# A hybrid encoder block on one core: cumulated decays loaded from DRAM to all partitions, in place of one-hot products

## The chip, the cores and the metric

The kernel runs on one core of one Trainium2 chip. The metric is the device time of one execution in microseconds (us). TensorE multiplies, VectorE and ScalarE work on SBUF and PSUM, GpSimd on SBUF alone, and SyncE (SP) issues nearly all DMAs, in order.

## The reference, cut to what matters

One layer over x of 512 positions by 1024 channels, float32. Beside a pooling branch, eight heads of a gated delta rule run forward and backward, each with its own decay; a convolutional feed-forward part follows.

```python
h = rmsnorm(x, norm1_w[l])
proj = h @ w_in[l]
p, q, k, v, z, bf, bb, af, ab, g_pool, g_dn = jnp.split(proj, SPLIT_POINTS, axis=-1)
...
g_f = -jnp.exp(a_l[0]) * jax.nn.softplus(af.astype(f32) + dtb[0])
g_b = -jnp.exp(a_l[1]) * jax.nn.softplus(ab.astype(f32) + dtb[1])
o_f = gated_delta_rule(qc, kc, vc, g_f, beta_f)
o_b = flip(gated_delta_rule(flip(qc), flip(kc), flip(vc), flip(g_b), flip(beta_b)))
...
# inside gated_delta_rule, by chunks
G = jnp.cumsum(g, axis=-1)
diff = G[..., :, None] - G[..., None, :]
decay = jnp.where(incl, jnp.exp(jnp.minimum(diff, 0.0)), 0.0)
attn = jnp.einsum('bhnid,bhnjd->bhnij', q, k) * decay
qg = q * jnp.exp(G)[..., None]
```

The kernel works with chunks of 128 positions, four to a direction. For each head and direction it needs G (the cumulated decay) of the column position in every row: a row of 512 numbers spread over 128 partitions.

## The kernel before, in words

**How the work is laid out.** Every step is declared as a task with an engine, an estimated cost, the names it reads and writes and a key (`A`, `V`, `G`, `M`, `L` for ScalarE, VectorE, GpSimd, TensorE and SP's loads). A planner (`Planner.run`) simulates the engines with these costs: at each moment an engine takes the ready task with the smallest key whose buffers are free, and a ScalarE task that would change the activation table stands back for 2.0 us. The order it finds is emitted as it stands, so a changed cost, buffer count or dependence re-orders the whole program. `RINGS` says how many buffers each ring has (`ds`: three PSUM banks for short products; `r4`: four SBUF tiles of 4 KB per partition; `q`, `v`, `f`, `ext` and more); rings in the second argument are handed out in the order of declaration. Weight work has the smallest keys (`FEED`), then evictions (`EVICT`), then the delta chain (`CHAIN`); projections with plain keys fill TensorE in between.

**Projections.** Each unit of 128 output columns loads 512 KB of weights, ScalarE rounds them to a high part (L393), GpSimd makes the low part (L397), and TensorE adds 8 x 3 products of 128 x 512 (`mm3`, L372 to L374): the split format, fp32r. Products of the delta chain are plain fp32, 128 columns each.

**The decays.** `gate_unit` cumulates the log decays with triangular matrices and keeps G by token (`g_all`), split into a high and a low part (`g_hl`, L670 and L671). Four transposes (`row_turn`, L677) and a copy to `g_rows` (L680) give 32 rows of 512 positions: 16 high, 16 low, one for each head and direction. `decay_unit` then spreads one row at a time to all partitions: a one-hot matrix `pick`, whose column r has ones at rows r and r + 16, is the weight (L711):

```python
pe.matmul(gb[d], pick[:, r : r + 1].to_broadcast([32, P]), g_rows, start=True, stop=True)
```

From this PSUM bank VectorE makes the argument of the decay for each chunk (L718: plus neg_g, at most the mask) into an `r4` tile, ScalarE makes the exponentials of G for the queries (`qexp`, L726) from the same bank, and the decays themselves in place (`dexp`, L729).

**What follows.** `mats_unit` multiplies k by k and by the decays (L836, L844) and stores 32 x 32 blocks to DRAM (L855); `inv_unit` inverts these blocks on VectorE, `spread_unit` loads them back, `merge_unit` joins them. `delta_unit` runs two heads and both directions in four steps (L1109 to L1170). `fin_unit` norms and gates a head's output and splits it into high and low parts (L1262, L1265). Heads 0 to 3 (group 0) go first, then heads 4 to 7, whose decays reuse the `r4` tiles of the first group. In between TensorE works on the z, q, v, k and gate projections. `p_unit` makes the pooled maps `pm` (in `r4` tiles, L1355), `po_unit` and `do_unit` the two output projections; then come `w_o`, the up projection and the down projection.

Of the kernel before, what the change touches and what calls it, by code (L numbers as in the profile page):

```python
# [14 lines left out]
P = 128  # L15
S = 512
# [21 lines left out]
class Planner:  # L38
# [48 lines left out]
    def run(self):  # L87
# [33 lines left out]
        while todo:  # L121
# [6 lines left out]
            while again:  # L128
                again = False
                for e, q in queue.items():  # L130
# [3 lines left out]
                    for t in q:  # L134
# [3 lines left out]
                        rank = (turn and now - t.ready < 2.0, t.key, t.i)  # L138
# [35 lines left out]
                    for s in t.succs:  # L174
# [4 lines left out]
                        if not n.left:  # L179
                            queue.setdefault(n.eng, []).append(n)  # L180
                            heapq.heappush(events, max(now, n.ready))
                            if n.tab:
                                heapq.heappush(events, n.ready + 2.0)
# [25 lines left out]
def hybrid_block(  # L209
# [33 lines left out]
        "pp": 3, "ds": 3, "oo": 1, "raw": 3, "whi": 2, "wlo": 2, "y": 5, "f": 5, "z": 1, "q": 4, "v": 3,  # L243
# [38 lines left out]
    def f32(ap):  # L282
        return ap.bitcast(F32)
# [24 lines left out]
    pick = const.tile([32, 16], F32R, name="pick")  # L308
    pool.tensor_tensor(out=pick, in0=ident[0:32, 0:16], in1=ident[0:32, 16:32], op=ALU.add)
# [163 lines left out]
    g_hl = tok.tile([P, 4, 2, 16], F32R, name="g_hl")  # L473
    g_rows = tok.tile([32, S], F32R, name="g_rows")
# [124 lines left out]
    def gate_unit(box, pp):  # L599
# [72 lines left out]
        V(0.85, keep, r=["ds:gsum"], w=["g_all", "g_hl"], key=c)  # L672
# [6 lines left out]
        M(0.5, row_turn, r=["g_hl"], w=["ds:grow"], key=c)  # L679
        A(ca(512), lambda: act.copy(g_rows, gt["pr"][0:32, :]), r=["ds:grow"], w=["g_rows"], key=c)  # L680
# [24 lines left out]
    def decay_unit(h, c):  # L705
        gb = [None, None]

        def spread(d):
            gb[d] = bank("ds", f"gb_{h}{d}")
            r = 2 * h + d  # L710
            pe.matmul(gb[d], pick[:, r : r + 1].to_broadcast([32, P]), g_rows, start=True, stop=True)  # L711

        def arg(d):
            if dts[h] is None:
                dts[h] = r4(f"dt_{h}")
            for t in range(NT):
# [13 lines left out]

# [1213 lines left out]
```

## Time and profile before

| what | us |
|---|---|
| median of 3 runs (902.24 to 907.81) | 902.29 |
| profiled execution | 903.34 |
| its span, from first to last instruction | 901.5 |
| TensorE busy in the span | 887.5 |
| VectorE / ScalarE / GpSimd busy | 539.4 / 458.9 / 503.2 |

Busy time counts a moment once however many matmuls are under way; a matmul's own duration is longer than the distance to the next one, since they are pipelined. Where the price of a matmul is wanted, the distance between starts is to be read.

### The profile page before, as it was taken

Reading aid. Unit: us, or ns where it says so; the run is one execution under the profiler, and the core shown is the slowest. Engines: PE = TensorE matmul, PEld = TensorE weight load, DVE = VectorE, ACT = ScalarE, POOL = GpSimd, SP = SyncE. Lnnn points to the kernel's source line nnn. Section 1 sums busy time; section 2 is a strip of 40 time slices with the busy share of each in tenths; the row PEclk is TensorE's granted clock in tenths of the full one; section 3 lists DMA queues with packets and bytes.
Section 4 is the critical chain, followed back from the end, with each engine's and each line's share of the span. In section 5 each row is a group of like instructions: output and inputs, shape, how many; then the busy total and the mean of one; then the engine's idle time right before and its main releaser. Section 6 shows DMA issues by size and latency. Waiting matters only on the chain.

```text
span 901.5 us, 14144 instructions
## 1 busy us (share of the span) xinstructions
PE 887.5 (98%) x5194; PEld 739.0 (82%) x5194; DVE 539.4 (60%) x985; ACT 458.9 (51%) x791; POOL 503.2 (56%) x452
## 2 busy tenths in 40 slices
PE   8999999999999999999999999999999999999997
PEld 7878888788888877988888888878888888888876
DVE  4766684338877845564234244665655554579996
ACT  6688534428777343355544333534443333455654
POOL 3434555124375451366567905787778774566663
PEclk9999999999999999999999999999999999999999
DMA  6333548122245381131898606566665563265554
GB/s 204 97 110 106 135 113 200 52 71 71 54 130 133 115 204 35 47 87 60 250 325 264 191 21 213 172 212 221 219 212 198 201 209 103 95 210 176 184 175 152
DMA packets 175033, 135.97 MB, mean 151 GB/s; under 512 B 31942, under 2 KB 143347, under 8 KB 174964
## 3 DMA queue, kind: packets, MB, share of 16 engines
q1 hardware_dynamic: 174388, 134.02, 48.6%
q8 instruction: 41, 0.67, 0.3%
q10 hardware_dynamic: 576, 1.05, 0.3%
q14 instruction: 28, 0.23, 0.1%
HBM read 109.88 MB, written 25.17 MB: 150 GB/s over the span
## 4 chain that ended last, share of the span: by engine, by line
PE 86%; DVE 4%; DMA 3%; POOL 2%; SPq 2%; issue 1%; ACT 1%; POOLq 0%; DVEq 0%; ACTq 0%
PE ps_up L373 8%; PE ps_up L374 8%; PE ps_up L372 8%; PE dn L373 3%; PE dn L374 3%; PE dn L372 3%; PE ps_gd L372 2%; PE ps_z L372 2%; PE ps_k L372 2%; PE ps_q L372 2%; PE ps_k L374 2%; PE ps_k L373 2%; PE ps_do L374 2%; PE ps_wo L374 2%; PE ps_wo L372 2%; PE ps_wo L373 2%
## 5 line engine op out<-in xcount | busy, mean ns | idle before, releaser
L397 POOL TENSOR_TENSOR wl_up<-wr_up,wh_up 128x512 fp32r<-128x512 f32 x88 | 114.8, 1326 | 51.0 <-ACT wh_up L393 48.6
L374 PE MATMUL ps_up<-h_hi,wl_up 128*128 128x512 f32 (+1 forms) x368 | 139.9, 380 | 1.0 <-POOL wl_up L397 1.0
L373 PE MATMUL ps_up<-h_lo,wh_up 128*128 128x512 f32 (+1 forms) x368 | 139.9, 380 | 0.3 <-DVE h_lo L543 0.3
L372 PE MATMUL ps_up<-h_hi,wh_up 128*128 128x512 f32 (+1 forms) x368 | 140.0, 380 | 0.0
L1665 DVE SCALAR_TENSOR_TENSOR c<-ps_up,fw,c 128x511 f32<-128x511 f32 x88 | 66.0, 750 | 98.7 <-ACT c L1659 92.6
L1846 POOL TENSOR_TENSOR w_dn<-wr_dn,w_dn 128x512 fp32r<-128x512 f32 x44 | 65.2, 1493 | 35.9 <-ACT w_dn L1843 33.5
L1650 POOL TENSOR_TENSOR tp<-tp 128x512 f32<-128x512 f32 x44 | 61.4, 1395 | 41.4 <-DMA tp<-in_ffn_down_dram 38.5
L374 PEld LDWEIGHTS ps_up<-h_hi,wl_up 128*128 128x128 f32 x368 | 69.2, 188 | 14.5 <-POOL wl_up L397 1.4
L373 PEld LDWEIGHTS ps_up<-h_lo,wh_up 128*128 128x128 f32 x368 | 69.2, 188 | 13.5 <-DVE h_lo L543 0.5
L372 PEld LDWEIGHTS ps_up<-h_hi,wh_up 128*128 128x128 f32 x368 | 69.2, 188 | 13.3
L393 ACT CAST wh_up<-wr_up 128x1024 fp32r<-128x1024 f32 x44 | 46.3, 1052 | 62.7 <-issue 21.8
L1843 ACT CAST w_dn<-wr_dn 128x512 fp32r<-128x512 f32 x69 | 40.4, 618 | 41.1 <-DMA wr_dn<-in_ffn_down_dram 16.9
L373 PE MATMUL dn<-w_dn,as 128*128 128x512 f32 x141 | 54.6, 387 | 2.0 <-DVE w_dn L1846 1.9
L374 PE MATMUL dn<-w_dn,as 128*128 128x512 f32 x141 | 54.2, 385 | 0.0
L372 PE MATMUL dn<-w_dn,as 128*128 128x512 f32 x141 | 54.2, 385 | 0.0
L1619 DVE TENSOR_TENSOR as<-a,as 128x512 fp32r<-128x512 f32 (+1 forms) x41 | 38.9, 983 | 1.4 <-ACT as L1615 1.4
L397 POOL TENSOR_TENSOR wl_gp<-wr_gp,wh_gp 128x512 fp32r<-128x512 f32 x16 | 21.2, 1346 | 33.2 <-ACT wh_gp L393 33.2
L1615 ACT CAST as<-a 128x512 fp32r<-128x512 f32 (+1 forms) x41 | 21.5, 534 | 29.1 <-DVE a L1686 28.3
L397 POOL TENSOR_TENSOR wl_k<-wr_k,wh_k 128x512 fp32r<-128x512 f32 x16 | 20.2, 1285 | 26.4 <-ACT wh_k L393 22.0
L397 POOL TENSOR_TENSOR wl_v<-wr_v,wh_v 128x512 fp32r<-128x512 f32 x16 | 20.3, 1293 | 24.4 <-ACT wh_v L393 24.4
L1659 ACT ACTIVATE c<-ps_up,fw 128x512 f32<-128x512 f32 x44 | 33.9, 771 | 0.0
L397 POOL TENSOR_TENSOR wl_do<-wr_do,wh_do 128x512 fp32r<-128x512 f32 x16 | 25.0, 1586 | 15.1 <-ACT wh_do L393 15.1
(357 smaller groups left out, 2443.9 us busy)
## 6 DMA issues: line engine op xcount, KB each, us to landing
wr_up<-in_ffn_up_dram SPq DMA_DIRECT2D x44, 512.0 KB, 3.8
tp<-in_ffn_down_dram SPq DMA_DIRECT2D x22, 512.0 KB, 5.3
t_scr<-tp SPq DMA_DIRECT2D x44, 256.0 KB, 3.0
wr_dn<-t_scr SPq DMA_DIRECT2D x20, 512.0 KB, 4.0
wr_dn<-in_ffn_down_dram SPq DMA_DIRECT2D x15, 512.0 KB, 3.7
x<-in_x_dram SPq DMA_DIRECT2D x8, 512.0 KB, 5.3
wr_k<-in_w_in_dram SPq DMA_DIRECT2D x8, 512.0 KB, 5.5
wr_z<-in_w_in_dram SPq DMA_DIRECT2D x8, 512.0 KB, 4.1
```

Source lines behind the costliest of these rows:

```text
L372: pe.matmul(ps, ahi, bhi, start=first, stop=False)
L373: pe.matmul(ps, ahi, blo, start=False, stop=False)
L374: pe.matmul(ps, alo, bhi, start=False, stop=last)
L393: act.copy(b["hi"], b["raw"])
L397: pool.tensor_tensor(out=b["lo"][:, sl], in0=b["raw"][:, sl], in1=f32(b["hi"][:, sl]), op=ALU.subtract)
L1615: act.copy(sets[p][:, i : i + n, 0, :], src())
L1619: dve.tensor_tensor(out=w[:, :, 1, :], in0=src(), in1=f32(w[:, :, 0, :]), op=ALU.subtract)
L1650: G(cp(512), lambda o=o, x=x, y=y: pool.tensor_tensor(out=w(*o), in0=w(*x), in1=w(*y), op=ALU.subtract), r=[n(*x), n(*y)], w=[n(*o)], key=u)
L1659: act.activation(b[j], box["ps"], AF.Identity, scale=fw[:, 1, ci : ci + 1], bias=fw[:, 3, ci : ci + 1])
L1665: dve.scalar_tensor_tensor(out=y[:, lo:hi], in0=box["ps"][:, lo + sh : hi + sh], scalar=fw[:, k, ci : ci + 1], in1=y[:, lo:hi], op0=ALU.mu ...
L1843: act.copy(b["w"][:, 0, :], raw["t"][:, j, :])
L1846: eng.tensor_tensor(out=b["w"][:, 1, :], in0=raw["t"][:, j, :], in1=f32(b["w"][:, 0, :]), op=ALU.subtract)
```

## The change: what it does

`g_hl`, `pick` and the one-hot products go. The four transposes turn `g_all` itself (16 rows); the copy goes to a tile of the `f` ring, from which SP stores the rows to DRAM (`g_scr2`, one store for the forward direction, four for the backward one, whose chunks are turned round). Each `decay_unit` then loads its head's two rows to all 128 partitions straight into the `r4` tile (512 KB); `qexp` reads that tile, and the argument overwrites it. Besides: `pm` 2 and 3 share a tile of the `ext` ring instead of `r4` tiles; heads 6 and 7 take their sums in `fin_unit` on VectorE instead of GpSimd; rings `f` 5 to 6, `q` 4 to 3, `v` 3 to 4; and the planner's delay of table changes is 3.0 instead of 2.0 us.

```diff
-                        rank = (turn and now - t.ready < 2.0, t.key, t.i)
+                        rank = (turn and now - t.ready < 3.0, t.key, t.i)
...
-        "pp": 3, "ds": 3, "oo": 1, "raw": 3, "whi": 2, "wlo": 2, "y": 5, "f": 5, "z": 1, "q": 4, "v": 3,
+        "pp": 3, "ds": 3, "oo": 1, "raw": 3, "whi": 2, "wlo": 2, "y": 5, "f": 6, "z": 1, "q": 3, "v": 4,
...
-    pick = const.tile([32, 16], F32R, name="pick")
-    pool.tensor_tensor(out=pick, in0=ident[0:32, 0:16], in1=ident[0:32, 16:32], op=ALU.add)
...
-    g_hl = tok.tile([P, 4, 2, 16], F32R, name="g_hl")
-    g_rows = tok.tile([32, S], F32R, name="g_rows")
+    g_scr2 = dram.tile([H, 2, NT, P], F32, name="g_scr2")
...
-            dve.tensor_copy(hl[:, :, 0, :, :], g_all)
-            dve.tensor_tensor(out=hl[:, :, 1, :, :], in0=g_all, in1=f32(hl[:, :, 0, :, :]), op=ALU.subtract)
...
-                pe.transpose(pt[0:32, s * P : (s + 1) * P], f32(g_hl[:, s]).rearrange("p x r -> p (x r)"), ident)
+                pe.transpose(pt[0:16, s * P : (s + 1) * P], g_all[:, s].rearrange("p h d -> p (h d)"), ident)
+
+        def store_rows():
+            g_rows = gt["g"]
+            for d in range(2):
+                for s in range(NT) if d else (None,):
+                    if d:
+                        sp.dma_start(g_scr2[:, d, NT - 1 - s, :], g_rows[d::2, s * P : (s + 1) * P])
+                    else:
+                        sp.dma_start(g_scr2[:, d].rearrange("h t c -> h (t c)"), g_rows[d::2, :])
...
+        A(ca(512), keep_rows, r=["ds:grow", "pool:dp"], w=["f:grows"], key=c)
+        add("sp", 2.2, store_rows, ["f:grows"], ["g_scr2"], c, None, 32.0)
...
-        def spread(d):
-            gb[d] = bank("ds", f"gb_{h}{d}")
-            r = 2 * h + d
-            pe.matmul(gb[d], pick[:, r : r + 1].to_broadcast([32, P]), g_rows, start=True, stop=True)
+        def spread():
+            dts[h] = r4(f"dt_{h}")
+            sp.dma_start(dts[h], g_scr2[h].partition_broadcast(P))
...
-                    out=dts[h][:, d, t, :], in0=gb[d][:, s * P : (s + 1) * P], scalar=neg_g[:, s, h, d : d + 1],
+                    out=dts[h][:, d, t, :], in0=dts[h][:, d, t, :], scalar=neg_g[:, s_of(d, t), h, d : d + 1],
...
-            act.activation(qes[h][:, d].rearrange("p s c -> p (s c)"), gb[d][:, P:], AF.Exp)
+            src = dts[h][:, 0, 1:4] if d == 0 else dts[h][:, 1, 2::-1]
+            act.activation(qes[h][:, d], src, AF.Exp)
...
+        L(512, spread, r=["g_scr2"], w=[f"r4:dt{h}"], key=c)
         for d in range(2):
-            M(0.35, lambda d=d: spread(d), r=["g_rows", "pool:dp"],
-              w=[f"ds:gb{h}{d}", f"r4:dt{h}#{d}", f"qe:{h}#{d}"], key=c)
-            V(4 * cd(128), lambda d=d: arg(d), r=[f"ds:gb{h}{d}", "neg_g"], w=[f"r4:dt{h}#{d}"], key=c)
-            A(ca(384), lambda d=d: qexp(d), r=[f"ds:gb{h}{d}", "pool:dp"], w=[f"qe:{h}#{d}"], key=c, tab="exp")
+            A(ca(384), lambda d=d: qexp(d), r=[f"r4:dt{h}#{d}", "pool:dp"], w=[f"qe:{h}#{d}"], key=c, tab="exp")
+            V(4 * (cd(128) + 0.12), lambda d=d: arg(d), r=["neg_g"], w=[f"r4:dt{h}#{d}"], key=c)
...
+        E, cost, eng = (G, cp(512), pool) if h < H - 2 else (V, cd(512), dve)
...
+    pmn = [f"ext:pm#{g}" if g > 1 else f"r4:pm{g}" for g in range(4)]
...
+            if g > 1:
+                if not pmx:
+                    pmx["t"] = ring("dp", "ext", (P, 2, 2, S), F32R, "pm_x")
+                pm[g] = pmx["t"][:, 3 - g]
+            else:
+                pm[g] = r4(f"pm_{g}", (P, 2, S), F32R)
```

## Rows read from the trace of the kernel before

**Rows 1.** Page, parts 1 and 2: busy us, share and count; granted clock.
```profile
PE 887.5 (98%) x5194; PEld 739.0 (82%) x5194; DVE 539.4 (60%) x985; ACT 458.9 (51%) x791; POOL 503.2 (56%) x452
...
PEclk9999999999999999999999999999999999999999
```

**Rows 2.** Three stretches: length, busy us and count by engine, clock, DMA share, GB/s.
```profile
0.00:25.00 25.00, 22.33 (x141) 19.20 (x141) 11.08 (x20) 15.24 (x30) 10.21 (x57) 0.93 0.61 186
25.00:875.00 850.00, 845.89 (x4944) 704.06 (x4944) 508.66 (x929) 432.35 (x740) 482.20 (x389) 1.00 0.49 149
875.00:901.50 26.50, 19.23 (x111) 15.78 (x109) 19.64 (x37) 11.29 (x22) 10.83 (x7) 0.98 0.49 166
```

**Rows 3.** TensorE's timeline, 49.4 to 52.3 us: start, duration, line, tiles, shape, count.
```profile
49.48 0.39 PE L374 MATMUL ps_z<-h_hi,wl_z 128*128 128x512 f32 x1
49.80 0.73 PE L711 MATMUL gb<-g_rows,pick 32*128 32x512 f32 x2
50.46 0.50 PE L372 MATMUL ps_z<-h_hi,wh_z 128*128 128x512 f32 x1
50.80 0.39 PE L373 MATMUL ps_z<-h_lo,wh_z 128*128 128x512 f32 x1
51.03 0.40 PE L374 MATMUL ps_z<-h_hi,wl_z 128*128 128x512 f32 x1
51.35 0.49 PE L711 MATMUL gb<-g_rows,pick 32*128 32x512 f32 x1
51.77 0.50 PE L372 MATMUL ps_z<-h_hi,wh_z 128*128 128x512 f32 x1
52.11 0.40 PE L373 MATMUL ps_z<-h_lo,wh_z 128*128 128x512 f32 x1
```

**Rows 4.** Tile gb: count, ns min/median/max, first and last start in us, shape.
```profile
L718 DVE SCALAR_TENSOR_TENSOR dt<-gb,neg_g,mask x64: 319/343/351, 51.0 to 253.4; 128x128 f32<-128x128 f32 x64
...
L711 PE MATMUL gb<-g_rows,pick x16: 392/490/497, 49.8 to 250.1; 32*128 32x512 f32 x16
```

**Rows 5.** TensorE's timeline behind plain fp32 products, near 63 and 67 us.
```profile
62.80 0.48 PE L372 MATMUL ps_q<-h_hi,wh_q 128*128 128x512 f32 x1
63.12 0.40 PE L373 MATMUL ps_q<-h_lo,wh_q 128*128 128x512 f32 x1
...
67.29 0.49 PE L711 MATMUL gb<-g_rows,pick 32*128 32x512 f32 x1
67.70 0.50 PE L372 MATMUL ps_z<-h_hi,wh_z 128*128 128x512 f32 x1
68.04 0.40 PE L373 MATMUL ps_z<-h_lo,wh_z 128*128 128x512 f32 x1
```

**Rows 6.** DMA issues: tiles, queue, count, size, median us to landing.
```profile
z_scr<-zo SPq DMA_DIRECT2D x8, 256.0 KB, 2.0
...
n2b<-in_norm_w_dram SPq DMA_DIRECT2D x1, 512.0 KB, 6.6
nfb<-in_final_norm_w_dram SPq DMA_DIRECT2D x1, 512.0 KB, 4.3
```

**Rows 7.** Tile dt: the users of the finished decays, and their exponentials.
```profile
L844 DVE SCALAR_TENSOR_TENSOR nm<-pk,nbp,dt x64: 333/342/353, 63.2 to 270.9; 128x128 f32<-128x128 f32 x64
L729 ACT ACTIVATE dt<-dt x16: 614/630/650, 56.3 to 259.5; 128x512 f32<-128x512 f32 x16
```

**Rows 8.** Tiles wr_v and ps_v: issue of v's weights, and their first products.
```profile
L388 SPq DMA_DIRECT2D wr_v<-in_w_in_dram x8: 368/378/390, 49.2 to 306.0; - x8
...
L372 PE MATMUL ps_v<-h_hi,wh_v x64: 388/389/486, 73.2 to 331.1; 128*128 128x512 f32 x64
```

**Rows 9.** TensorE's timeline: last products of the second delta pair.
```profile
241.04 1.06 PE L1170 MATMUL o<-dt,w 128*128 128x128 f32 x8
```

**Rows 10.** Tile ob: a VectorE instruction with two operands in SBUF.
```profile
L1252 DVE SCALAR_TENSOR_TENSOR ob<-ob,small,zs x8: 744/1043/1798, 202.9 to 424.4; 128x512 f32<-128x512 f32 x8
```

**Rows 11.** Tile o_lo: a head's low part, and the output projection that reads it.
```profile
L373 PE MATMUL ps_do<-o_lo,wh_do x64: 389/389/398, 452.8 to 496.0; 128*128 128x512 f32 x64
L1265 POOL TENSOR_TENSOR o_lo<-ob,o_hi x8: 1272/1289/1760, 222.5 to 436.3; 128x512 fp32r<-128x512 f32 x8
```

More of the change, by code (lines that the diff above doesn't have):

```diff
@@ L182, in run @@
                             if n.tab:
-                                heapq.heappush(events, n.ready + 2.0)
+                                heapq.heappush(events, n.ready + 3.0)
         return sorted(ts, key=lambda t: (t.start, t.i))
@@ L676, in row_turn, with keep_rows @@
             for s in range(4):
-                pe.transpose(pt[0:32, s * P : (s + 1) * P], f32(g_hl[:, s]).rearrange("p x r -> p (x r)"), ident)
-        M(0.5, row_turn, r=["g_hl"], w=["ds:grow"], key=c)
-        A(ca(512), lambda: act.copy(g_rows, gt["pr"][0:32, :]), r=["ds:grow"], w=["g_rows"], key=c)
+                pe.transpose(pt[0:16, s * P : (s + 1) * P], g_all[:, s].rearrange("p h d -> p (h d)"), ident)
[7 more added lines that the diff above has]
+                        sp.dma_start(g_scr2[:, d].rearrange("h t c -> h (t c)"), g_rows[d::2, :])
+        M(0.5, row_turn, r=["g_all"], w=["ds:grow"], key=c)
+        def keep_rows():
+            gt["g"] = ring("dp", "f", (16, S), F32, "g_rows")
+            act.copy(gt["g"], gt["pr"][0:16, :])
+        A(ca(512), keep_rows, r=["ds:grow", "pool:dp"], w=["f:grows"], key=c)
+        add("sp", 2.2, store_rows, ["f:grows"], ["g_scr2"], c, None, 32.0)
         def rest():
@@ L1230, in fin_unit @@
         A(ca(512), square, r=[n("o")], w=[n("sq")], key=c)
-        G(cp(512), lambda: pool.tensor_tensor(out=b["sq"], in0=b["sq"], in1=b["a"], op=ALU.add),
-          r=[n("a")], w=[n("sq")], key=c)
+        E, cost, eng = (G, cp(512), pool) if h < H - 2 else (V, cd(512), dve)
+        E(cost, lambda: eng.tensor_tensor(out=b["sq"], in0=b["sq"], in1=b["a"], op=ALU.add), r=[n("a")], w=[n("sq")], key=c)
         def part():
@@ L1239, in rest @@
             b["lo"] = f_tile("osl", F32R)
-            pool.tensor_tensor(out=b["lo"], in0=b["sq"], in1=f32(b["hi"]), op=ALU.subtract)
+            eng.tensor_tensor(out=b["lo"], in0=b["sq"], in1=f32(b["hi"]), op=ALU.subtract)
         def total():
@@ L1247, in fin_unit @@
         A(ca(512), part, r=[n("sq")], w=[n("hi")], key=c)
-        G(cp(512), rest, r=[n("sq"), n("hi")], w=[n("lo")], key=c)
+        E(cost, rest, r=[n("hi"), n("sq")], w=[n("lo")], key=c)
         M(0.55, total, r=[n("hi"), n("lo")], w=[f"ds:pm{h}"], key=c)
@@ L1269, in hybrid_block @@
     pm = [None] * 4
+    pmx = {}
+    pmn = [f"ext:pm#{g}" if g > 1 else f"r4:pm{g}" for g in range(4)]
     def p_unit(g):
@@ L1350, in pmap @@
             mm3(b["p2"], b["w"][:, 0], b["w"][:, 1], b["yhi"], b["ylo"], True, True)
-        M(MM3, pmap, r=[f"pwr:{g}", f"y:yh{g}", f"y:yl{g}"], w=[f"ds:pw{g}", f"r4:pm{g}"], key=u)
+        M(MM3, pmap, r=[f"pwr:{g}", f"y:yh{g}", f"y:yl{g}"], w=[f"ds:pw{g}", pmn[g]], key=u)
         def sc_hi():
-            pm[g] = r4(f"pm_{g}", (P, 2, S), F32R)
+            if g > 1:
[4 more added lines that the diff above has]
+                pm[g] = r4(f"pm_{g}", (P, 2, S), F32R)
             act.activation(pm[g][:, 0, :], b["p2"], AF.Copy, scale=small[:, g : g + 1])
@@ L1362, in sc_lo @@
             )
-        A(ca(512), sc_hi, r=[f"ds:pw{g}", "small"], w=[f"r4:pm{g}"], key=u)
-        V(cd(512), sc_lo, r=[f"ds:pw{g}"], w=[f"r4:pm{g}"], key=u)
+        A(ca(512), sc_hi, r=[f"ds:pw{g}", "small"], w=[pmn[g]], key=u)
+        V(cd(512), sc_lo, r=[f"ds:pw{g}"], w=[pmn[g]], key=u)
     def po_unit(c):
@@ L1369, in po_unit @@
             pool_out[0][:, c * P : (c + 1) * P], 4, lambda k: (pm[k][:, 0, :], pm[k][:, 1, :]),
-            lambda k, a, b_: [f"r4:pm{k}"], f"po{c}",
+            lambda k, a, b_: [pmn[k]], f"po{c}",
         )
@@ L1597, in hybrid_block @@
     tail = [b for b in plan.owner if b.split(":")[0] == "y" or b[:3] in ("mhi", "mlo", "woh", "wol") or b[:2] in ("kT", "kk")]
-    tail += [n for n in ("beta", "xg", "neg_g", "neg_eg", "kdec", "gl", "g_rows", "g_hl")]
+    tail += [n for n in ("beta", "xg", "neg_g", "neg_eg", "kdec", "gl")]
     Z(ffn_open, w=["pool:fp"], after=tail)
```

7 lines of the change are left out of this document (1 added, 6 removed).

## The prediction

> **What bounds the kernel.** I read the page's busy shares first, then the stretches, then single matmuls. TensorE is busy 887.5 of 901.5 us, VectorE 60%, ScalarE 51%, GpSimd 56% [rows 1], and its granted clock stands at the higher of its levels (2.4 GHz) in nearly every slice. A busy share alone proves little, since busy time of pipelined matmuls overlaps; so the reader should see where the 14.0 us of idle time lie. By the three stretches [rows 2] 2.7 us lie in the first 25 us (the start: loads, first norm), 7.3 us after 875 (last matrix weights and the tail), and only 850.0 - 845.9 = 4.1 us in the 850 us between. In that long middle TensorE's queue is full. A second check is the distance between starts: matmuls of 512 columns follow each other every 0.23 us (50.80 to 51.03 [rows 3]). So a microsecond of matmul work taken from the middle is a microsecond of time, as long as the remaining work is there when its turn comes, and an engine beside it matters only if it makes TensorE wait.
>
> **What the change removes from TensorE.** The one-hot products: sixteen matmuls (8 heads, 2 directions) of 32 rows by 512 columns, between 49.8 and 250.1 us [rows 4]. Their own duration (0.49) is not their price; the distances are. One alone [rows 3]: its predecessor starts at 51.03, it at 51.35, the next product at 51.77, the one after at 52.11. From 51.03 to 52.11 are 1.08 us where two ordinary steps take 0.46: price 0.62. The queue loses 0.09 before it, 0.19 in it and 0.11 in the product behind it. A pair [rows 3]: 49.48 to 50.80 is 1.32, less 0.46, so 0.86 for two. One that follows another plain fp32 product [rows 5]: from its start at 67.29 to the second start after it, 68.04, are 0.75; less one step of 0.23, and less the 0.09 that a change from fp32 to the split format costs even without it (62.80 to 63.12 is 0.32, not 0.23), leaves 0.43. The timeline has eleven alone, one behind fp32 work, and two pairs, the second of them behind fp32 work (0.65 by the same reduction): 11 x 0.62 + 0.43 + 0.86 + 0.65 = 8.8 us. The four transposes that turn the cumulated decays into rows stay (16 columns each where 32 were), and nothing is added to TensorE. Sum on TensorE: -8.8 us.
>
> A page of the notes says otherwise. The Trainium skill, TensorE: Matmul & The Clock Gate, Why this matters for your kernels, holds that a single matmul over 32 rows takes as long as one over 128; by that each product costs one step of 0.23, the sixteen 3.7 us, and the time would be 898.6. The same skill's TensorEngine Tiling (Array Packing), Key Properties, says that a change of tiling mode drains the engine, which agrees with the 0.09 and 0.11 lost on either side. Measured distances decide for 0.62.
>
> **What it adds, and what covers it.** Five small stores on SP (one of 16 KB, four of 4 KB), then eight loads that copy a head's two 2 KB rows to 128 partitions, 512 KB each. No such load is in the trace before. The nearest rows are the two norm weights spread by the same kind of load: 4.3 and 6.6 us to landing; a store takes 2.0 [rows 6]; an issue on SP some 0.3 to 0.6. Group 0 (heads 0 to 3): rows ready at 49.5 by the first product's start; five issues 2.5, landing 2.0, issue 0.4, load 4.3 to 6.6 put the first decays at 58.7 to 61.0, where before they stood in PSUM at 50.3: 8.4 to 10.7 us later. Heads follow at the rate of the queue. The first use of a finished decay is at 63.2 [rows 7], so the first mats may slip a few us; but the fourth head's mats wait for its own k product late in the stage, so the inversion starts when it did. I take 0 for group 0; the bound is the full 10.7. While SP stands at the wait for the five stores, weight loads queue behind it. Their cover: the weights of the first v product are issued at 49.2 and first multiplied at 73.2 [rows 8], so a hold of 5 us costs 0. Without that cover a late weight load would stop TensorE for as long as it is late.
>
> Group 1 (heads 4 to 7): the buffer of the third pair comes free when the second delta pair ends, near 242.1 (241.04 + 1.06 [rows 9]). With issue and load, heads 6 and 7 have theirs at 246.8 to 249.1 instead of the first product at 243.4. ScalarE's query exponentials now stand before VectorE's decay arguments, because those overwrite the loaded tile: some 0.5 us more per direction. The last decay exponential starts at 259.5 and the last mats at 270.9 [rows 7], which leaves some 10 us of cover. I take 0, with 12 us as the bound of the delay.
>
> VectorE's 64 arguments (0.343 each [rows 4]) now read two operands in SBUF rather than one in PSUM. The nearest row with two SBUF operands, of 512 columns, runs from 0.744 to 1.798 [rows 10], a factor of 2.4. Bounds: 0, or 64 x 0.343 x 1.4 = 31 us of VectorE time over both groups; VectorE is 60% busy, and I take a third of it, hidden. The Trainium skill, SBUF — State Buffer, Who interferes with whom, gives the reason to expect the upper part: a Vector instruction with two SBUF inputs contends with a GpSimd instruction that reads SBUF. The spread of that row agrees.
>
> The eight loads move 4.2 MB; the queues are half used in the middle (DMA share 0.49 [rows 2]): 0.
>
> **What it moves.** Last two heads' squares and splits go from GpSimd to VectorE, the first two mapped pool groups into the freed `ext` buffer, a fourth v slot for a q slot, a sixth f slot, and the planner waits 3 rather than 2 us before it changes the activation table. None changes TensorE's work. They matter through the slack at the end of the delta stage: the last head's low part is done at 436.3 + 1.3 = 437.6, its consumer's stage begins at 452.8 [rows 11], and it is needed some 21 products (4.8 us) later. With TensorE 8.8 us earlier that slack is still 452.8 + 4.8 - 8.8 - 437.6 = 11 us. I take 0 for all; they re-lay the whole order, so the 4.1 us of idle in the middle may double or vanish, which is the main uncertainty: +-4.1.
>
> **Sum.** Profiled execution 903.34 (span 901.5): -8.8 gives 894.5. It lies 1.05 above the median 902.29, so against the median 893.5. From the idle in the middle I take 0.3 off (pool maps no longer wait for decay buffers): 893.2.
>
> **Rivals.**
> 1. The re-laid order gives back what was won: new waits of about 4 to 5 us, that is, the idle of the middle doubled. For: the planner re-times every engine with estimated costs, and loads that it cannot time exactly enter the chain. Against: TensorE has work queued throughout. Time 893.2 + 4.5 = 897.7.
> 2. A product is worth only its step and the drains turn up elsewhere: 16 x 0.23 = 3.7 us, so 902.29 - 3.7 = 898.6. For: the new order may put other changes of format where the products stood. Against: the distances of [rows 3] hold the drains beside the products. The page on the clock gate cited above stands for this case.
> 3. Slower: the delay of the decay chain reaches the end of the delta stage. Mechanism: loads on SP and slower arguments start the inversions late, o's last head arrives late, TensorE stands in front of the output projection. Price: delay D less the 11 us of slack; it decides from D = 20, where 893.2 + 9 is the time before. Only both groups at their upper bounds, adding up (10.7 + 12 = 23 us), give 893.2 + 12 = 905. Against: group 0's delay should end at the k products.
> 4. The order gets better: the 4.1 us of idle in the middle go: 889.4.
>
> **How the numbers follow.** Forecast 0.68 (its own range 890 to 896.5, with idle and drains a few us either way), rival 1 0.15, rival 2 0.05, rival 3 0.07, rival 4 0.05. A measurement of this kernel tells about 1% from no change, that is 893.3 or less is faster: half of the forecast's weight and rival 4 lie below, so faster 0.50; same takes the other half, rivals 1 and 2: 0.43; slower, rival 3: 0.07. Range 888.8 to 899.5: both bounds of the idle time, and rivals 1, 2 and 4, without 3.
>
> **What would show it.** Right: no products with 32 rows; the starts of the neighbouring products 0.23 apart there; TensorE's busy time near 878.5; idle in the middle near 4; eight loads of 512 KB landing in 4 to 7 us; the first output-projection product near 444. Wrong: TensorE idle before the merges or the output projection with a load, a decay or a late head as its releaser; weight loads that land after their turn; or the same busy time with more changes of format.

## The result, and the profile after

The changed kernel takes 897.89 us (median of 7 runs, 896.0 to 899.66) against 902.29 us: a ratio of 0.9936, interval 0.9915 to 0.9957. That is 4.4 us less, where the forecast said 9.1. The profiled execution took 899.28 us, 1.4 above its median. By the page (busy us, share, count) and the three stretches of [rows 2]:

```profile
PE 877.8 (98%) x5178; PEld 737.0 (82%) x5178; DVE 557.0 (62%) x987; ACT 462.3 (52%) x793; POOL 498.2 (56%) x447
```

```profile
0.00:25.00 25.00, 22.21 (x143) 19.59 (x144) 11.07 (x20) 15.42 (x31) 10.25 (x57) 0.93 0.64 186
25.00:875.00 850.00, 840.09 (x4941) 704.05 (x4941) 531.25 (x941) 438.89 (x747) 480.76 (x387) 1.00 0.52 155
875.00:897.60 22.60, 15.51 (x97) 13.33 (x95) 14.70 (x28) 7.99 (x16) 7.20 (x5) 0.98 0.43 152
```

TensorE has 9.7 us less to do (887.5 in [rows 1]) and 16 matmuls fewer, but the span fell by 3.9 only, because its idle time rose from 14.0 to 19.8. Almost all of that stands in the long middle: 4.1 before, 850.00 - 840.09 = 9.9 now. To place it, take stretches that begin and end with the same work in both kernels: from the first row transpose to the first product of the output projection, and the last stage (the down projection). Before:

```profile
45.80:452.60 406.80, 405.01 (x2915) 337.41 (x2914) 244.70 (x588) 227.97 (x410) 190.65 (x176) 1.00 0.41 111
786.20:896.00 109.80, 107.11 (x496) 87.91 (x495) 95.91 (x124) 63.30 (x121) 68.31 (x46) 1.00 0.55 181
```

After:

```profile
45.60:446.20 400.60, 395.86 (x2899) 335.28 (x2898) 260.68 (x591) 225.93 (x407) 184.85 (x171) 1.00 0.47 125
779.40:891.70 112.30, 107.12 (x496) 87.78 (x494) 97.58 (x124) 64.21 (x121) 67.98 (x46) 1.00 0.54 177
```

The first stretch, which holds all that was changed, has 9.15 us less TensorE work (405.01 - 395.86) and 2.95 us more idle time (1.79 to 4.74), so it is 6.2 shorter. Between the two stretches 0.4 was won (333.6 to 333.2). The last stage has the same TensorE work, and 2.5 us more idle time. With -0.2 ahead of the first stretch and +0.4 behind the last one: -0.2 - 6.2 - 0.4 + 2.5 + 0.4 = -3.9, the span's change. So there are two losses, one beside the change and one that begins 333 us behind the end of the first stretch.

What ended TensorE's idle times in the changed kernel (the waits of TensorE: waiting tile and line, releaser, us in total, times, longest). `rw` is what VectorE hands to the products `pw` and `su` in each step of the delta chain, `l1a` and `l1b` are products of the merges, `dn` is the down projection:

```profile
PE dn L371 <- DVE w_dn L1857: 3.9, 2, 2.3
...
PE l1a L958 <- DMA ext<-e_scr: 1.2, 1, 1.2
PE su L1150 <- ACT o_hi L1265: 1.2, 1, 1.2
PE dn L371 <- POOL wt_lo L1857: 1.1, 1, 1.1
PE l1b L969 <- DMA nm<-u_scr: 1.1, 1, 1.1
...
PE ps_do L372 <- POOL wl_do L395: 0.8, 1, 0.8
PE pw L1135 <- DVE rw L1115: 0.6, 1, 0.6
PE su L1150 <- DVE rw L1139: 0.3, 1, 0.3
```

Four kinds: the last stage waits for low parts of weights (dn), merges for their block loads (l1a, l1b: 2.3 us), the delta chain for VectorE (su, pw: 2.1), the output projection for a weight's low part (0.8; it lies behind the first stretch). None names a decay or its load. The three waits of the delta chain are, all the same, the change's own. VectorE's timeline of the changed kernel (start, duration, line, operation, tiles, shape, count) shows why:

```profile
228.06 5.85 DVE L720 SCALAR_TENSOR_TENSOR dt<-dt,neg_g,mask 128x128 f32<-128x128 f32 x8
233.83 3.09 DVE L752 SCALAR_TENSOR_TENSOR cv_q<-ps_q,cw,cv_q 128x510 f32<-128x510 f32 x4
236.84 1.12 DVE L1115 SCALAR_TENSOR_TENSOR rw<-ks,neg_eg,v 128x128 f32<-128x128 f32 x4
237.87 3.20 DVE L720 SCALAR_TENSOR_TENSOR dt<-dt,neg_g,mask 128x128 f32<-128x128 f32 x4
241.00 0.68 DVE L1258 TENSOR_TENSOR ob<-ob,osq 128x512 f32<-128x512 f32 x1
241.60 0.68 DVE L1139 TENSOR_TENSOR rw<-pw,bkd 128x512 f32<-128x512 f32 x1
```

Four arguments take 3.20 us here; four of the kernel before take 1.09. Eight stand ahead of the first `rw` and four ahead of the second, and TensorE's timeline has the products that need them right behind:

```profile
238.02 1.16 PE L1135 MATMUL pw<-rw,nm 128*128 128x128 f32 x8 [0.64 <-DVE rw L1115]
...
242.42 1.13 PE L1150 MATMUL su<-rw,ktok 128*128 128x128 f32 x8 [1.18 <-ACT o_hi L1265]
```

The first starts when `rw` (L1115) ends at 237.96. The second is put down to ScalarE's `o_hi`; its operand `rw` (L1139) ended at 241.60 + 0.68 = 242.28, only 0.05 before `o_hi`. And `o_hi` was late for the same reason, as ScalarE's timeline has it:

```profile
241.71 0.62 ACT L1265 CAST o_hi<-ob 128x512 fp32r<-128x512 f32 x1 [2.99 <-DVE ob L1258]
```

It stood for `ob`, which VectorE makes directly behind the four arguments. The wait's name points at the last semaphore, not at the cause; the cause is further up in VectorE's queue.

The decays themselves, by tile dt (count, ns min/median/max, first and last start):

```profile
L720 DVE SCALAR_TENSOR_TENSOR dt<-dt,neg_g,mask x64: 339/345/1431, 58.0 to 272.7; 128x128 f32<-128x128 f32 x64
L846 DVE SCALAR_TENSOR_TENSOR nm<-pk,nbp,dt x64: 337/340/354, 69.2 to 285.5; 128x128 f32<-128x128 f32 x64
...
L716 SPq DMA_DIRECT2D dt<-g_scr x8: 319/358/431, 51.9 to 253.3; - x8
...
DMA to landing us min/median/max: 5.5/5.9/6.4
```

Against [rows 4] and [rows 7]: the first argument 7.0 us later (51.0 to 58.0), the first mats 6.0 later (63.2 to 69.2), the last mats 14.6 later (270.9 to 285.5). Everything behind follows: the first merge product starts 6.3 us later (156.0 to 162.3) and the last delta product 17.1 later (413.5 to 430.6), though TensorE has less to do.

### The profile page after: what moved, and what is told of

Same layout as the page of the kernel before. It is cut to its first block, busy times and chain, and to the rows that moved or that the text cites. A ratio compares the mean times of both kernels' runs of the same rounds, so it can differ in the third digit from the quotient of the medians.

```text
span 897.6 us, 14100 instructions
## 1 busy us (share of the span) xinstructions
PE 877.8 (98%) x5178; PEld 737.0 (82%) x5178; DVE 557.0 (62%) x987; ACT 462.3 (52%) x793; POOL 498.2 (56%) x447
## 4 chain that ended last, share of the span: by engine, by line
PE 82%; DVE 8%; DMA 3%; issue 2%; SPq 1%; ACT 1%; POOL 1%; POOLq 0%; DVEq 0%; ACTq 0%
PE ps_up L371 9%; PE ps_up L372 9%; PE ps_up L370 9%; PE ps_do L372 2%; PE ps_wo L370 2%; PE ps_wo L371 2%; PE ps_wo L372 2%; PE ps_z L372 2%; PE ps_z L371 2%; PE ps_z L370 2%; DVE as L1630 2%; PE ps_do L371 2%; PE ps_do L370 2%; PE ps_k L370 2%; PE ps_v L370 2%
## 5 line engine op out<-in xcount | busy, mean ns | idle before, releaser
L395 POOL TENSOR_TENSOR wl_up<-wr_up,wh_up 128x512 fp32r<-128x512 f32 x88 | 113.4, 1310 | 52.3 <-ACT wh_up L391 50.1
L371 PEld LDWEIGHTS ps_up<-h_lo,wh_up 128*128 128x128 f32 x368 | 69.2, 188 | 13.8 <-DVE h_lo L540 0.5
L372 PEld LDWEIGHTS ps_up<-h_hi,wl_up 128*128 128x128 f32 x368 | 69.2, 188 | 13.2
L370 PEld LDWEIGHTS ps_up<-h_hi,wh_up 128*128 128x128 f32 x368 | 69.2, 188 | 13.0
L1626 ACT CAST as<-a 128x512 fp32r<-128x512 f32 (+1 forms) x41 | 21.5, 534 | 29.9 <-DVE a L1697 28.6
L395 POOL TENSOR_TENSOR wl_q<-wr_q,wh_q 128x512 fp32r<-128x512 f32 x16 | 20.3, 1292 | 29.8 <-ACT wh_q L391 26.1
L371 PEld LDWEIGHTS dn<-w_dn,as 128*128 128x128 f32 x141 | 26.5, 188 | 11.1 <-DVE w_dn L1857 5.2
L1857 DVE TENSOR_TENSOR w_dn<-wr_dn,w_dn 128x512 fp32r<-128x512 f32 x25 | 26.2, 1048 | 10.4 <-ACT w_dn L1854 10.4
L1699 ACT ACTIVATE c<-c 128x512 f32<-128x512 f32 x22 | 13.9, 633 | 35.6 <-DVE c L1676 35.6
```

What stands on the lines that cost most here:

```text
L370: pe.matmul(ps, ahi, bhi, start=first, stop=False)
L371: pe.matmul(ps, ahi, blo, start=False, stop=False)
L372: pe.matmul(ps, alo, bhi, start=False, stop=last)
L395: pool.tensor_tensor(out=b["lo"][:, sl], in0=b["raw"][:, sl], in1=f32(b["hi"][:, sl]), op=ALU.subtract)
L1626: act.copy(sets[p][:, i : i + n, 0, :], src())
L1857: eng.tensor_tensor(out=b["w"][:, 1, :], in0=raw["t"][:, j, :], in1=f32(b["w"][:, 0, :]), op=ALU.subtract)
```

## The experiments

Ratios are against the kernel before, run on the same chip, with 95% intervals. "Row stretch" is the first of the two stretches above, from the row transposes to the output projection.

### The price on TensorE

**Only the products go (e10_no_products).** The kernel before, in its old order, with nothing where the one-hot products stood.

```diff
-            gb[d] = bank("ds", f"gb_{h}{d}")
-            r = 2 * h + d
-            pe.matmul(gb[d], pick[:, r : r + 1].to_broadcast([32, P]), g_rows, start=True, stop=True)
+            pass
...
-out=dts[h][:, d, t, :], in0=gb[d][:, s * P : (s + 1) * P], scalar=...
+out=dts[h][:, d, t, :], in0=ones, scalar=...
...
-act.activation(qes[h][:, d].rearrange("p s c -> p (s c)"), gb[d][:, P:], AF.Exp)
+act.activation(qes[h][:, d].rearrange("p s c -> p (s c)"), ones[:, 0:1].to_broadcast([P, 3 * P]), AF.Exp)
```

> The kernel before with its planned order and costs, but the sixteen products are not issued; the argument and the queries' exponential read a constant SBUF tile instead of their bank (so the cumulated decays are left out). Theory F: the products alone are worth 8.8 us of TensorE's time and the old order keeps the rest, so that TensorE's idle time before the output projection stays below 3 us, its first product stands 8 to 9.5 us earlier than before (443 to 444.5), and the time is 893.5 to 895.5: what the change lacks was given back by its new order and loads. Rival: the old order also gives 3 to 5 us back as waits once TensorE is faster, 897 to 899.

896.29 us, ratio 0.9919 (0.9898 to 0.9941). Its row stretch, in the windows:

```profile
47.80:447.00 399.20, 396.52 (x2899) 335.25 (x2898) 254.19 (x588) 227.87 (x410) 192.96 (x176) 1.00 0.41 114
```

Work 405.01 to 396.52 is -8.5 us (8.8 forecast), length 406.8 to 399.2 is -7.6, idle 2.68. So the prediction's price of the products holds, and in the old order some 0.9 of it is lost to idle. The time stays above the 893.5 to 895.5 that was expected. The whole run gained 0.81%, 7.3 us on 902.29: so much is taking the products away worth in the old order, with arguments that now read SBUF. The change got 4.4; the two intervals overlap.

**The same products with 128 rows (e1_rows128).** `pick` and `g_rows` get 128 rows, the added ones zero; nothing else.

```diff
-    pick = const.tile([32, 16], F32R, name="pick")
+    pick = const.tile([P, 16], F32R, name="pick")
...
-    g_rows = tok.tile([32, S], F32R, name="g_rows")
+    g_rows = tok.tile([P, S], F32R, name="g_rows")
...
-            pe.matmul(gb[d], pick[:, r : r + 1].to_broadcast([32, P]), g_rows, start=True, stop=True)
+            pe.matmul(gb[d], pick[:, r : r + 1].to_broadcast([P, P]), g_rows, start=True, stop=True)
```

> The kernel before with its one-hot products over 128 rows instead of 32 (the added rows are zero); everything else and the order of all engines stay. Theory A, a product costs 0.62 us because the array is set from 128 to 32 rows and back: the products then cost one step of 0.23 each, the distances on both sides fall to 0.23, TensorE's busy time falls by about 16 x 0.62 - 16 x 0.23 less what pairs share, some 5 us, and the time is 897. Rival, the price lies in the one-hot weights themselves (one column repeated 128 times) or in the waits beside them: distances stay at 1.08 for two steps and the time at 902.3.

898.07 us, ratio 0.9952 (0.9937 to 0.9968). TensorE's timeline of this kernel, the place of [rows 3]:

```profile
50.03 0.40 PE L374 MATMUL ps_z<-h_hi,wl_z 128*128 128x512 f32 x1
50.27 0.39 PE L712 MATMUL gb<-g_rows,pick 128*128 128x512 f32 x1
50.50 0.39 PE L372 MATMUL ps_z<-h_hi,wh_z 128*128 128x512 f32 x1
50.73 0.39 PE L373 MATMUL ps_z<-h_lo,wh_z 128*128 128x512 f32 x1
```

The starts are 0.23 apart before, in and behind the product. With four times the rows it costs 0.23 where it cost 0.62, and TensorE's work in the row stretch falls by 5.3 (405.01 to 399.70). The loss of [rows 3] went with the 32 rows. That it is paid for the change between 32 and 128 rows, and not for each product, is argued from the pair of [rows 3]: its second product adds one step only (0.86 - 0.62). And the order stays as it was: idle in the row stretch is 1.2 us. This edit of a few lines, without a load from DRAM, cannot be told from the whole change by its time: the two intervals overlap.

### The change, halved

**The loads alone (e2_loads_only).** Before, with the decays by stores and loads; rings, pooled maps, last heads' sums and table delay as they were.

```diff
...
-            pe.matmul(gb[d], pick[:, r : r + 1].to_broadcast([32, P]), g_rows, start=True, stop=True)
+            sp.dma_start(dts[h], g_scr2[h].partition_broadcast(P))
...
```

> The kernel before with the loads from DRAM alone: rings, pooled maps, the last heads' engines and the delay of table changes as before. Theory B, the loads and the slower arguments bring back by themselves what the products gave: TensorE busy 9 us less, idle of its middle 4 to 6 us more, 897 to 899. Rival, the rearrangements beside the loads cost the time: 893, with the idle of the middle near 4 us.

898.97 us, ratio 0.9958 (0.9944 to 0.9973). Row stretch 402.2 us with 5.41 idle; the waits again name `rw` (VectorE, 2.1 and 0.8 us) and the merges' block loads (1.6). So the loads bring both the gain and the loss.

**The rest alone (e3_rest_only).** After, with `g_hl`, `pick` and the one-hot products back, and five `f` buffers.

```diff
...
-            sp.dma_start(dts[h], g_scr2[h].partition_broadcast(P))
+            pe.matmul(gb[d], pick[:, r : r + 1].to_broadcast([32, P]), g_rows, start=True, stop=True)
...
```

> The changed kernel with the one-hot products put back (and five f slots): rearrangements alone. Theory B: as before within 2 us, 900 to 904. Rival, the rearrangements cost what is missing: 906 to 907, with 4 us more idle in TensorE's middle.

904.26 us, ratio 1.0013 (0.9999 to 1.0027); row stretch 407.6 with 2.23 idle. Pooled maps, rings, sums and table delay are worth nothing to the time by themselves.

### What the chain waits for

**The argument's operand (e5_sbuf_arg).** Before, with the argument's first operand from SBUF, the products left in place.

```diff
-out=dts[h][:, d, t, :], in0=gb[d][:, s * P : (s + 1) * P], scalar=...
+out=dts[h][:, d, t, :], in0=ones, scalar=...
```

> The kernel before, only that the argument of the decay takes its first operand from a constant tile in SBUF instead of the PSUM bank (so the decays themselves are left out); TensorE, ScalarE, GpSimd and SP keep their order and their work. Theory C, two SBUF operands make VectorE wait for GpSimd: the argument's mean goes from 344 ns to 500 to 560, and where it stands ahead of the delta chain's work TensorE waits 1 to 2.5 us more in the middle, 903 to 905. Rival, the changed kernel's longer arguments are only hidden and its waits come from late loads: same mean or not, time within 0.7 us of 902.3.

904.32 us, ratio 1.0018 (1.0004 to 1.0031). The argument's group in the lines view (busy us, mean ns of one) of the kernel before:

```profile
L718 DVE SCALAR_TENSOR_TENSOR dt<-gb,neg_g,mask 128x128 f32<-128x128 f32 x64 | 17.4, 344 | 2.3 <-PE gb L711 1.6 <-issue 0.7
```

of this kernel:

```profile
L718 DVE SCALAR_TENSOR_TENSOR dt<-ones,neg_g,mask 128x128 f32<-128x128 f32 x64 | 23.6, 438 | 0.0
```

and of the changed kernel:

```profile
L720 DVE SCALAR_TENSOR_TENSOR dt<-dt,neg_g,mask 128x128 f32<-128x128 f32 x64 | 30.2, 539 | 2.6 <-ACT qe L729 2.6
```

One operand moved to SBUF makes the mean 438 rather than 344 ns, with nothing else altered (500 to 560 had been expected). The mean hides two kinds. In the changed kernel 45 of the 64 arguments run with no GpSimd instruction beside them, and none of these takes over 0.36 us. All 13 that take over 0.8 us run beside one. In this kernel it is the same: 6 are lengthened, all beside one. In the kernel before, where the operand is in PSUM, 20 run beside GpSimd and none takes over 0.36. The four of 3.20 us above met this one (GpSimd's timeline of the changed kernel):

```profile
238.31 2.61 POOL L395 TENSOR_TENSOR wl_gd<-wr_gd,wh_gd 128x512 fp32r<-128x512 f32 x2 [5.60 <-ACT wh_gd L391]
```

So an argument from SBUF is slow where it meets GpSimd. Yet idle in the row stretch stays at 1.68 us here (1.79 before): in the old order the slower arguments cost TensorE nothing. What costs is not the slow argument alone but what the planner puts behind it.

**A shorter argument in the changed kernel's order (e9_no_mask).** One tile operand instead of two.

```diff
-                dve.scalar_tensor_tensor(
-                    out=dts[h][:, d, t, :], in0=dts[h][:, d, t, :], scalar=neg_g[:, s_of(d, t), h, d : d + 1],
-                    in1=mask[:, d, :], op0=ALU.add, op1=ALU.min,
+                dve.tensor_scalar(
+                    out=dts[h][:, d, t, :], in0=dts[h][:, d, t, :], scalar1=neg_g[:, s_of(d, t), h, d : d + 1],
+                    scalar2=0.0, op0=ALU.add, op1=ALU.min,
```

> The changed kernel, only that VectorE's argument adds the row's decay and takes the minimum with 0 in one instruction with one SBUF operand (the causal mask is left out); the order of all engines stays. Theory C, the argument held up by GpSimd stands ahead of the delta chain's work on VectorE: its 64 instructions shrink from 30.2 us to under 16, TensorE's three waits between 225 and 243 us (2.2 us together) fall below 0.5, and the time falls by 1.5 to 2.5 against the changed kernel (895.5 to 896.5 where that is 898). Rival, those waits come from the late decays themselves or from ScalarE: they stay within 0.7 us of 2.2 although the argument is short.

897.36 us, ratio 0.9931 (0.9907 to 0.9955); the changed kernel beside it 898.29. Its waits in the row stretch are the merges' alone:

```profile
PE l1a L958 <- DMA ext<-e_scr: 1.7, 1, 1.7
PE l1b L969 <- DMA nm<-u_scr: 0.7, 1, 0.7
```

All three waits of the delta chain for VectorE are gone, and idle there is 2.69 us instead of 4.26 in the changed kernel's profile of the same chip. The four arguments ahead of the second `rw` now end before GpSimd's next low parts begin (237.83 and 237.96), and take 0.86 us instead of 3.20:

```profile
236.97 0.86 DVE L720 TENSOR_SCALAR dt<-dt,neg_g 128x128 f32<-128x128 f32 x4
```

That shows the cause of those 2 us. The time itself fell by 0.9 us, less than was expected, and the intervals overlap. The arguments are also not as short as expected:

```profile
L720 DVE TENSOR_SCALAR dt<-dt,neg_g x64: 271/277/1342, 59.0 to 269.1; 128x128 f32<-128x128 f32 x64
```

The median fell to 277 ns, but 11 still take 0.79 to 1.34 us with one tile operand in SBUF, all beside a GpSimd instruction, and the mean is 442. The theory that two operands are needed for the slowdown does not hold; it is another kind of instruction, though: the `scalar_tensor_tensor` of the kernel before has one tile operand in SBUF and one in PSUM, and none of those was slow.

**The arguments off VectorE (e8_bias).** GpSimd puts the mask in, and the exponential adds `neg_g` as its bias.

```diff
...
-            V(4 * (cd(128) + 0.12), lambda d=d: arg(d), r=["neg_g"], w=[f"r4:dt{h}#{d}"], key=c)
-            A(ca(512), lambda d=d: dexp(d), r=[f"r4:dt{h}#{d}"], w=[f"r4:dt{h}#{d}"], key=c, tab="exp")
+            G(cp(512), lambda d=d: cover(d), w=[f"r4:dt{h}#{d}"], key=c)
+            A(4 * 0.24, lambda d=d: dexp(d), r=["neg_g"], w=[f"r4:dt{h}#{d}"], key=c, tab="exp")
```

> The changed kernel without VectorE's argument: GpSimd puts -30000 in the places that the mask cuts, and ScalarE adds the row's decay as the bias of the exponential (four short instructions for one long). Theory C: VectorE loses 30 us, TensorE waits for it below 0.7 us in the delta stage; ScalarE gains some 8 us and GpSimd some 20, which have room: 895 to 897. Rival, GpSimd's added work delays the weights' low parts and the chain: 898 to 901.

898.89 us, ratio 0.9947 (0.9929 to 0.9965). VectorE has 30 us less to do in the row stretch (260.68 to 231.06), no chain product there waits for `rw`, and idle is still 3.80: three waits of the merges for their loads, 2.5 us, stand in its place. In this new order, relieving an engine that is not the bottleneck bought nothing.

**Merges later (e6_late_merge).** The planner is told that a block load takes longer, so that it plans merges later.

```diff
-            L(128, lambda b_=b_: load(b_, True), ...
-            L(128, lambda b_=b_: load(b_, False), ...
+            L(256, lambda b_=b_: load(b_, True), ...
+            L(256, lambda b_=b_: load(b_, False), ...
```

> The changed kernel, only that the planner counts the loads of the inverted blocks at double size, so that it puts the merges behind them later. Theory D, the waits of TensorE for these loads (1.1 and 1.2 us in the changed kernel, 0.3 before) come from the planner's too early merges: they fall below 0.5 together and the time falls by about 2 us (the order changes, so 1 us either way). Rival, they come from loads that land later with the decay loads in the queues, in whatever order: waits of 2 us stay.

898.13 us, ratio 0.9932 (0.9911 to 0.9953), the same as the changed kernel. The load waits went, and the new order has others in the row stretch, 3.87 us idle in all:

```profile
PE pk L838 <- ACT osq L1253: 2.0, 1, 2.0
PE ps_p L370 <- ACT sgp L1200: 1.1, 1, 1.1
```

**The true cost of an argument (e12_arg_cost).** The planner adds 0.21 us per argument instead of 0.12, nearer to what is measured in the changed kernel.

```diff
-            V(4 * (cd(128) + 0.12), lambda d=d: arg(d), r=["neg_g"], ...
+            V(4 * (cd(128) + 0.21), lambda d=d: arg(d), r=["neg_g"], ...
```

> The changed kernel, only that the planner is told what an argument of the decays took here (0.54 us instead of 0.45). If its wrong estimate makes VectorE late for the delta chain, the three waits of 2.2 us fall below 0.7 and the time to about 896. Rival, the estimate is not the point and the new order waits elsewhere: 897.5 to 899.

902.5 us, ratio 0.9991 (0.9976 to 1.0006): the whole gain is gone. TensorE's work is what it was in the changed kernel, but the row stretch has 6.95 us idle, with waits of the same kinds and a new one for ScalarE (`pkq`):

```profile
PE l1a L958 <- DMA ext<-e_scr: 2.8, 3, 1.7
PE pw L1135 <- DVE rw L1115: 2.2, 1, 2.2
...
PE pkq L1058 <- ACT qT L764: 1.3, 1, 1.3
```

A truer cost did not give a better order here. I read each re-planning as another draw; this one loses as much as the change had won.

### The last stage

**The changed kernel again (after_again).** No edit.

> The changed kernel once more, without an edit, for a second profile. Theory E, part of what was lost comes from how VectorE and GpSimd happen to meet at their shared operand port in the last stage, whose order of work is that of the kernel before: TensorE's idle time there (5.1 us in the first profile, 2.5 before) differs between two profiles of the same kernel by over 0.7 us, and the waits before the output projection (4.7 us) stay within 0.5. Rival, the order fixes both: each within 0.5 us of the first profile.

898.29 us, ratio 0.9938 (0.9913 to 0.9962). The two stretches:

```profile
47.80:447.70 399.90, 395.64 (x2899) 335.21 (x2898) 260.61 (x591) 226.35 (x407) 184.90 (x171) 1.00 0.46 125
780.80:892.00 111.20, 106.96 (x496) 87.84 (x494) 98.46 (x124) 64.34 (x121) 67.40 (x46) 1.00 0.54 178
```

The row stretch repeats itself: idle 4.26 (4.74 in the first profile), with the same waits. The last stage does not: 4.24 after 5.18, with other releasers; 1.4 us are now put down to a small VectorE tile, `fst`, and 1.0 rather than 3.9 to `w_dn`. From the first to the last product of the down projection the order of the work on TensorE, VectorE and GpSimd is the same before, after and in all experiments but e13, yet its idle time is 2.69 before, 2.36 in e5, 2.73 in e2, 3.51 in e1, 4.23 in e10, 4.38 in e3. One VectorE row shows the sort of thing that differs, with GpSimd's row beside it. Before:

```profile
860.75 0.68 DVE L1846 TENSOR_TENSOR w_dn<-wr_dn,w_dn 128x512 fp32r<-128x512 f32 x1
860.86 1.72 POOL L1846 TENSOR_TENSOR w_dn<-wr_dn,w_dn 128x512 fp32r<-128x512 f32 x1 [0.92 <-DVE as L1619]
```

After (first profile):

```profile
854.80 1.75 DVE L1857 TENSOR_TENSOR w_dn<-wr_dn,w_dn 128x512 fp32r<-128x512 f32 x1
```

and GpSimd in the same profile of after:

```profile
854.46 1.54 POOL L1857 TENSOR_TENSOR w_dn<-wr_dn,w_dn 128x512 fp32r<-128x512 f32 x1 [0.46 <-ACT w_dn L1854]
```

The same subtraction takes 0.68 us where it starts 0.11 us ahead of GpSimd's, and 1.75 where GpSimd's has started 0.34 us ahead of it and runs until 856.0. Lengthened subtractions are not more frequent in the changed kernel: the 28 subtractions of this kind on VectorE take 28.6 us in all before, 29.3 and 28.0 in its two profiles. Which of them are slow depends on when each engine comes to them, and some have TensorE behind them. I read the 1.5 to 2.5 us lost here as such a shift of phase; the order argues for it, but no run set the phase on purpose, so it stays argued.

**Another split of the low parts (e13_lows).** After, with another share of the down weights' low parts on VectorE.

```diff
-            if k % 3 == 0:
+            if k % 4 == 3:
```

> The changed kernel, only that in the last stage VectorE makes the low part of two of eleven weight tiles instead of four (GpSimd the rest). Theory G: TensorE's idle time of the last stage (4.2 and 5.1 us in two profiles of the changed kernel) comes from low parts queued on a full VectorE behind instructions that wait for GpSimd: it falls below 3 us and the time by 1 to 2 us, to 896.5. Rival, GpSimd's added work makes its own low parts late: the idle time stays at 4 us or grows, 898 or more.

903.78 us, ratio 1.0004 (0.9993 to 1.0016). The row stretch stays (399.7); the last stage grew:

```profile
778.80:895.00 116.20, 110.57 (x496) 88.74 (x494) 90.14 (x109) 62.07 (x120) 87.01 (x59) 0.99 0.52 168
```

GpSimd has 59 instructions instead of 46 and idle is 5.63. Moving work from VectorE to GpSimd does not mend the stage; it loses 4 us more. Most of that is not idle time: the same 496 matmuls are busy for 110.57 us instead of 107.12. Part of it is the clock. After 2.5 us in which TensorE was busy for 1.07, the granted clock is 0.50 (the 1.2 GHz level), and products of 512 columns start 0.43 us apart instead of 0.23:

```profile
887.50:890.00 2.50, 2.50 (x10) 2.21 (x10) 1.15 (x1) 0.72 (x1) 2.31 (x2) 0.50 0.64 240
```

### A version between the two

**Heads 0 to 3 by loads, 4 to 7 by products of 128 rows (e11_hybrid).**

```diff
...
-        decay_unit(h, CHAIN + 5 * h)
+        decay_load(h, CHAIN + 5 * h)
```

> The kernel before with the decays of heads 0 to 3 loaded from DRAM as in the change and those of heads 4 to 7 spread by one-hot products over 128 rows. If the loads of the second group and the arguments beside its delta stage are what gives back most, this gains the full price of eight products (4.6 us), 3.2 us of the others, and loses some 1.5 us to waits: 896. Rival, any new order loses 3 us or more whatever it holds: 898 to 899.

912.64 us, ratio 1.0108 (1.0081 to 1.0136): the slowest kernel of the study. Its row stretch has TensorE work of 403.81 us and 13.99 us idle. The largest of its waits:

```profile
PE l1a L1008 <- DMA ext<-e_scr: 5.9, 3, 3.4
```

The merges of group 1 stand in front of their loads while the queues are full. The windows of that place (DMA share and GB/s last, clock before them):

```profile
355.00:357.50 2.50, 0.22 (x2) 0.14 (x2) 0.00 (x0) 0.00 (x0) 0.00 (x0) 1.00 1.06 172
357.50:360.00 2.50, 0.00 (x0) 0.00 (x0) 0.00 (x0) 0.00 (x0) 0.00 (x0) 0.83 1.22 271
360.00:362.50 2.50, 1.61 (x32) 1.32 (x33) 0.00 (x0) 0.27 (x1) 0.00 (x0) 0.50 0.37 62
362.50:365.00 2.50, 2.50 (x37) 1.56 (x41) 0.00 (x0) 0.56 (x1) 0.00 (x0) 0.50 0.00 0
```

From 355 to 360 us nearly everything stands still (TensorE is busy for 0.22 us in all) and only DMAs run. No version here clearly beats the changed kernel: the lowest ratios (e10, e9, e6) have intervals that overlap its own.

## Why the prediction was right or wrong

**The price of the products: right.** 8.8 us forecast; 9.15 less work in the changed kernel's row stretch, 8.5 in e10. The busy time came to 877.8 (near 878.5 forecast), and the output projection's first product with a low part to 446.5 (444). The distances beside the product were the right reading: e1 takes them to 0.23 by adding rows alone. By the rule of the Trainium skill that was weighed (TensorE: Matmul & The Clock Gate, Why this matters for your kernels) a single matmul of 32 rows takes as long as one of 128. This case's trace differs for one among matmuls of 128 rows: 0.62 against 0.23 by the distances. Rival 2 falls.

**Group 0's delay taken at 0, "because the fourth head's mats wait for its own k product": this step failed.** The delay was forecast at 8.4 to 10.7 us and came to 7.0 at the first argument; the loads landed in 5.5 to 6.4, in the expected 4 to 7. But the fourth head's k product did not cover it: the first merge started 6.3 later.

**Group 1's delay taken at 0 under "some 10 us of cover": failed too.** The last mats came 14.6 us later, above the bound of 12. No wait names a decay; the lateness is handed down the chain to the last delta product, 17.1 us later. What either delay cost in time no run singles out.

**The slow arguments, "a third, hidden": size right, cover wrong.** A third of 31 us is 10; measured 64 x (0.539 - 0.344) = 12.5. The reason that the Trainium skill gives (SBUF — State Buffer, Who interferes with whom), two SBUF inputs against a GpSimd instruction that reads SBUF, agrees with the trace: the place of the operand alone adds 0.09 us per argument (e5), and every slow argument runs beside GpSimd. For `tensor_scalar`, the instruction of e9, the same section says that it can enter a mode with two ports, and then can contend too; its 11 lengthened instructions agree, and in which mode they ran no run shows. What the prediction did not ask is what stands behind an argument in VectorE's queue: `rw`, then TensorE. Some 2 us.

**The delta stage's slack of 11 us (rival 3): the delay came, the price did not.** D was 17, so by the rival's sum 6 us should have been lost at the output projection. The list of waits has 0.8 there, for a weight's low part and not for a late head. What failed is the "some 21 products later" of the old order. In the new one VectorE takes up the first finished column block of the output projection (`gdl`, L1498) at 456.0, 9.8 us after the first product, and the second at 457.4; before, the first came 6.1 us after it (458.7 - 452.6). So other products stood in front of the last head's, whose low part was done only at 454.4 (437.6 before). Rival 3 falls as a mechanism of the end, while its delay is real.

**The moved parts and SP's hold at 0: right.** e3 gives +0.1% for the former, and no wait names one of v's weights.

**The idle of the middle, -0.3 with ±4.1: the step that made the number wrong.** Taken at the centre, it came to +2.95 in the row stretch, and +2.5 (first profile) or +1.5 (second) in the last stage. Over the long middle idle went from 4.1 to 9.9, beyond the 8.2 of the stated bound. Three additions of this change (loads in the chain, longer arguments, a later chain) all push towards more waits, and only the 0.3 of the pool maps the other way; where all known pushes have one sign, the centre is the wrong value to take. By its mechanism this is rival 1 (order re-laid, 4 to 5 us given back, 897.7), which had a chance of 0.15 and hit 897.89. That its price could appear also in a stage with an unchanged order was in no case. The range (888.8 to 899.5) held the time, in part by luck: the idle time left its bound, TensorE's work fell by 9.7 instead of 8.8, and the two misses partly cancel. (Its lower end seems to take the 0.3 of the pool maps twice: 893.2 - 4.1 is 889.1.)

**What the runs leave.** Of the 4.74 us idle in the row stretch (first profile), 2.1 are shown to be VectorE's arguments ahead of the chain (e9). Another 2.3 are merges that wait for their loads; that the planner put them too early is supported by e6, where they vanish, but e6 has another order throughout and idles elsewhere instead. The cause of the last stage's part is argued only.

## What to carry to other kernels

Before replacing an operation on the bottleneck engine, look at the distances between starts beside it: here the price came mostly from 32 rows among 128, and zero rows up to 128 won back 5.3 of some 9 us without touching the order. Where a planner re-lays everything, count what an edit adds to each queue in front of chain work and expect the new order to lose a few microseconds: here the row stretch idled 1.2 to 2.7 us in the old order, 2.2 to 5.4 in five new ones, 7 and 14 in the two worst. And read a wait's releaser as the last event only: the late instruction may stand ahead of it, in the queue of another engine.

## What the runs showed of the hardware that was not expected

- A matmul of 32 rows among ones of 128 rows costs 0.62 us, the same with zero rows added 0.23.
- A 128x128 VectorE instruction with operands in SBUF runs at its normal time (median 345 ns) where no GpSimd instruction runs beside it, and can take up to 1.43 us where one does: one row of eight took 5.85 us. With a single tile operand (`tensor_scalar`) the largest was still 1.34 us. With one operand in PSUM none of 64 was slowed.
- A load that copies 4 KB to all 128 partitions (512 KB) lands in 5.5 to 6.4 us, close to one of the two norm weights of [rows 6] (6.6).
- In e11, after those 5 us with almost no matmul, the granted clock fell to 0.50 (the 1.2 GHz level; 360 to 362.5 us) and was still there from 362.5 to 365 us, though TensorE was busy for all of that time. What that added was not measured.
